# A hybrid decoder layer on one core: sums of activations spread over a product, rotary tables in pieces in a slab of plain products, and turnings at the ends of stages placed between products

## The chip, the cores and the metric

The kernel runs on one core of one Trainium2 chip. The metric is the device time of one execution in microseconds, as the median over several executions. The kernel before takes 1881.18 us (three runs, 1879.79 to 1882.1).

## The reference

One layer on 256 tokens of width 2048, all in fp32, with a feed-forward part ("FFN") at either end:

```
x1 = x  + 1/2 * SwiGLU_1(RMSNorm(x))          # hidden width 5632
h  = RMSNorm(x1);  P = h @ w_in               # one projection for three groups of heads
     A: gated linear attention (4 heads)      B: sparse attention (8 heads, rotary, gathered blocks)
     C: cross attention into 256 memory tokens (4 heads)
x2 = x1 + concat(A, B, C) @ w_out
x3 = x2 + 1/2 * SwiGLU_2(RMSNorm(x2))
y  = RMSNorm(x3)

def swiglu(x, w_gate, w_up, w_down):
    return (jax.nn.silu(x @ w_gate) * (x @ w_up)) @ w_down
```

## The kernel before

**Stages.** First FFN, the mix (the three groups of heads), the output projection, second FFN. The weights come in from memory once, as pieces of 128x1024 in fp32 (tile `r`, a pool `raw` of 11). `split` (L283 to L290) cuts each into a high part, a copy to fp32r by ScalarE (`h`, L288), and a low part, a subtraction by VectorE (`l`, L289). Each product is then three matmuls, high with high, high with low, low with high (`mm3`, L301 to L304). So each piece of weights costs ScalarE a copy, VectorE a subtraction, and TensorE 6 or 12 matmuls of 128x512.

**An FFN.** The hidden width is cut into 11 slabs of 512. Slab 0 (`first_slab`, L404) makes the gate product and the up product plainly: 8 pieces of 12 matmuls each, for both halves of the tokens. Between the two stands `combine` (L352 to L379): it makes from the activations `hh`, `hl` the four sums that the later slabs multiply (tiles `sh`, `sl`): four adds (`whole`, L360), four sums of those (L369, L372, L374, L377), and four splits of the result (copy L365, subtraction L366), each on 128x1024. Slabs 1 to 10 (`slab`, L438) do three quarters of their depth as seven products in place of eight (`SEVENS` = 3: sums of weights by VectorE, L481, L483, L485, and an adding DMA on GpSimd's queue, L473) and one quarter plainly; that is 25 steps and 174 matmuls a slab, with VectorE putting blocks together afterwards (L493 to L496, L506, L508, L510, L512) and the activation at L507, L509, L511, L513.

**What is filled in.** The down product of slab s-1 runs inside slab s. After steps 2 and 4 (`TURNS`) the hidden values are turned (`hidden`, L388: four transposes L391, a copy L393 to the high part of `gx`, a subtraction L394 to its low part). After the steps listed in `FILLS` come eight "fills" of 12 matmuls each (L425), all into one PSUM bank `px`, each followed by an add to `acc` on VectorE (L402). In slab 10 the last two fills (`LATE` = 2) come after the slab's own products; then the hidden values of slab 10 itself are turned, and its down product runs plainly (L531 to L549).

**What else stands there.** `prepare` (L573) makes the rotary tables with some sixty small VectorE operations of 128x192 (L587 to L604), 128x128 and 128x64 (L613 to L615); it is called once, after step 10 of slab 1. After each quarter j of the width of the first FFN's last down product, and of the output projection, `square_acc` (L342) sums squares on ScalarE, and `transposed` (L334) turns that quarter of `acc` (transposes L339, split L330 and L331) into the input of the next stage (`xh`, `xl` for the mix, whose first product is `agq`, L688; `zh`, `zl` for the second FFN).

**Order.** Each engine runs its instructions in one fixed order. A scheduler fixes it when the program is built: it goes by the program's order as a priority, and by its own estimate of when an instruction could start. A wait at the head of an engine's order holds up all behind it.

## Time and profile before

| | |
|---|---|
| median of three runs | 1881.18 us (1879.79 to 1882.1) |
| the profiled execution | 1881.27 us, of which the span in the profile is 1879.5 us |
| TensorE busy | 1840.5 us, 98% of the span |
| VectorE busy | 1642.3 us, 87% |
| ScalarE busy | 1086.0 us, 58% |
| GpSimd busy | 84.6 us, 5% |
| read from memory | 393.68 MB, 211 GB/s over the span |

Busy means that at least one instruction of the engine was running. TensorE is cut in two: PE is the matmul itself, PEld the load of its weights, which overlaps. Matmuls overlap each other too: one lasts about 0.39 us, and the next starts before it ends. A stretch in which TensorE counts as busy all the time can still be slow where the granted clock is low.

### The profile page before, as it was taken

What the parts mean: (1) busy time and instruction counts of PE and PEld (TensorE: products, weight loads), DVE (VectorE), ACT (ScalarE), POOL (GpSimd) and SP (SyncE); (2) the same over time, 40 slices, a digit from 0 to 9 for tenths busy, and PEclk for the clock granted to TensorE, in tenths of its full rate; (3) what the DMA queues carried; (4) which work ended last, traced back from release to release, by engine and by line L of the source; (5) the groups of instructions that cost most, each with busy time, mean ns of one, the idle gap of its engine ahead of it and who ended that gap; (6) DMA issues with size and microseconds to landing.
All of it is one profiled execution on the core that took longest, in us unless ns stands there. A gap on an engine that the chain in (4) does not pass through costs nothing.

```text
span 1879.5 us, 23784 instructions
## 1 busy us (share of the span) xinstructions
PE 1840.5 (98%) x8465; PEld 1486.1 (79%) x8465; DVE 1642.3 (87%) x2101; ACT 1086.0 (58%) x1376; POOL 84.6 (5%) x109
## 2 busy tenths in 40 slices
PE   8989999999999999999999999999999999999997
PEld 5868888888888877777777787888888888888885
DVE  7999999999999985576577854999999999999995
ACT  7446665656565656533456744566556655666563
POOL 0000000000000000001010000000000000000000
PEclk9999999999999999999999999999999999999999
DMA  9768777767776754545744453876777677767771
GB/s 333 228 190 261 253 225 235 247 202 226 236 249 197 229 169 158 188 150 177 247 157 130 163 181 117 295 239 209 213 237 255 203 214 238 253 201 216 239 246 49
DMA packets 111655, 397.34 MB, mean 211 GB/s; under 512 B 12592, under 2 KB 12848, under 8 KB 111408
## 3 DMA queue, kind: packets, MB, share of 16 engines
q1 hardware_dynamic: 102896, 364.36, 55.4%
q0 software_dynamic: 8640, 31.46, 9.7%
q8 instruction: 66, 1.08, 0.2%
q14 instruction: 53, 0.43, 0.1%
HBM read 393.68 MB, written 2.10 MB: 211 GB/s over the span
## 4 chain that ended last, share of the span: by engine, by line
PE 91%; DVE 5%; ACT 1%; issue 1%; POOL 1%; ACTq 0%; POOLq 0%; DVEq 0%
PE pm L303 20%; PE pm L302 20%; PE pm L304 20%; PE px L303 8%; PE px L302 8%; PE px L304 8%; DVE l L289 1%; PE pt L391 1%; PE pm L854 1%; PE px L819 0%; POOL y L326 0%; PE pt L339 0%; DVE exg L910 0%; PE po L1047 0%; POOL y L325 0%
## 5 line engine op out<-in xcount | busy, mean ns | idle before, releaser
L288 ACT ACTIVATE h<-r 128x1024 fp32r<-128x1024 f32 (+1 forms) x838 | 877.8, 1052 | 660.3 <-PE pm L304 491.6
L289 DVE TENSOR_TENSOR l<-r,h 128x1024 fp32r<-128x1024 f32 (+1 forms) x838 | 990.7, 1207 | 137.7 <-ACT h L288 129.3
L303 PE MATMUL px<-l,gx 128*128 128x512 f32 x624 | 243.2, 390 | 1.7 <-DVE l L289 1.7
L302 PE MATMUL px<-h,gx 128*128 128x512 f32 x624 | 243.2, 390 | 0.0
L304 PE MATMUL px<-h,gx 128*128 128x512 f32 x624 | 242.9, 389 | 0.0
L303 PE MATMUL pm<-l,sh 128*128 128x512 f32 x480 | 191.9, 400 | 2.3 <-DVE l L289 2.3
L302 PE MATMUL pm<-h,sh 128*128 128x512 f32 x480 | 190.1, 397 | 0.3 <-ACT h L288 0.3
L304 PE MATMUL pm<-h,sl 128*128 128x512 f32 x480 | 188.0, 392 | 0.0
L303 PE MATMUL pm<-l,hh 128*128 128x512 f32 x364 | 144.8, 398 | 3.6 <-DVE l L289 3.6
L302 PE MATMUL pm<-h,hh 128*128 128x512 f32 x364 | 142.4, 395 | 4.4 <-ACT h L288 4.4
L303 PE MATMUL pm<-l,zh 128*128 128x512 f32 x364 | 144.3, 396 | 0.1
L302 PE MATMUL pm<-h,zh 128*128 128x512 f32 x364 | 143.3, 394 | 0.0
L304 PE MATMUL pm<-h,zl 128*128 128x512 f32 x364 | 142.2, 391 | 0.0
L304 PE MATMUL pm<-h,hl 128*128 128x512 f32 x364 | 142.2, 391 | 0.0
L303 PEld LDWEIGHTS px<-l,gx 128*128 128x128 f32 x624 | 117.2, 188 | 26.7 <-DVE l L289 2.4
L302 PEld LDWEIGHTS px<-h,gx 128*128 128x128 f32 x624 | 117.2, 188 | 25.4 <-ACT h L288 0.2
L304 PEld LDWEIGHTS px<-h,gx 128*128 128x128 f32 x624 | 117.2, 188 | 24.2
L303 PE MATMUL pm<-l,xh 128*128 128x512 f32 (+2 forms) x320 | 120.7, 377 | 1.5 <-DVE l L289 1.5
L302 PE MATMUL pm<-h,xh 128*128 128x512 f32 (+2 forms) x320 | 121.3, 380 | 0.0
L304 PE MATMUL pm<-h,xl 128*128 128x512 f32 (+2 forms) x320 | 121.0, 379 | 0.0
L402 DVE SCALAR_TENSOR_TENSOR acc<-px,acc 128x512 f32<-128x512 f32 x156 | 106.9, 685 | 8.3 <-PE px L304 7.9
L302 PEld LDWEIGHTS pm<-h,sh 128*128 128x128 f32 x480 | 90.6, 189 | 20.5 <-ACT h L288 0.9
(329 smaller groups left out, 2641.0 us busy)
## 6 DMA issues: line engine op xcount, KB each, us to landing
r<-ffn1u SPq DMA_DIRECT2D x88, 512.0 KB, 4.9
r<-ffn1d SPq DMA_DIRECT2D x88, 512.0 KB, 4.9
r<-ffn2u SPq DMA_DIRECT2D x88, 512.0 KB, 4.7
r<-ffn2d SPq DMA_DIRECT2D x88, 512.0 KB, 4.8
r<-ffn1g SPq DMA_DIRECT2D x87, 512.0 KB, 5.0
r<-ffn2g SPq DMA_DIRECT2D x87, 512.0 KB, 5.1
r<-wout SPq DMA_DIRECT2D x32, 512.0 KB, 3.4
r<-ffn1u POOLq DMA_DIRECT2D x30, 512.0 KB, 7.3
```

Source lines behind the costliest of these rows:

```text
L288: act.activation(h[:, sl], r[:, sl], AF.Copy)
L289: dve.tensor_sub(l[:, sl], r[:, sl], f(h[:, sl]))
L302: pe.matmul(out, ah, wh, start=first, stop=False)
L303: pe.matmul(out, ah, wl, start=False, stop=False)
L304: pe.matmul(out, al, wh, start=False, stop=last)
L391: pe.transpose(pt[:, k], g[:, k * 128:k * 128 + 128], ident)
L402: dve.scalar_tensor_tensor(a, pd, 0.5, a, op0=ALU.mult, op1=ALU.add)
L854: pe.matmul(pcs[n][32 * p:32 * p + 32], flats[n][:, c * 4 + p], r[:, p * 256:p * 256 + 256], start=c == 0, stop=c == 7, tile_position=(0, ...
```

## The change

1. `combine` gives out its work as eight steps, and `product` calls one before each of the eight pieces of the up product, in both FFNs.
2. Slab 1 of the first FFN is made plain (`plain=(1,)`, no sevens): 16 steps of 12 matmuls, no sums of weights, no adding DMAs, and at its end two activations straight from PSUM and two multiplications. Its turnings and fills have their own places (`PLAIN_TURNS`, `PLAIN_FILLS`).
3. `prepare` is a generator, and one piece of it is called after each step of slab 1.
4. In slab 10 three fills are late, and the two turnings stand between them; the turned values go into a tile "gl" of their own in place of `gx`.
5. The sums of squares and the turning of the last quarter (j = 3), with the norm that needs it, move into the next stage's first product, before its piece 1.

```diff
-LATE = 2
+LATE = 3
+PLAIN_TURNS = (1, 2)
+PLAIN_FILLS = (3, 5, 6, 8, 9, 11, 12, 14)
...
-        def whole(k0, t0):
-            x = raw().rearrange("p (k t) -> p k t", k=8)
+        x = {}
+
+        def whole(n, k0, t0):
+            x[n] = raw().rearrange("p (k t) -> p k t", k=8)
             q = (slice(None), slice(k0, k0 + 8), slice(t0, t0 + 128))
-            dve.tensor_add(x, f(th[q]), f(tl[q]))
-            return x
-
-        def put(i, x):
+            dve.tensor_add(x[n], f(th[q]), f(tl[q]))
+
+        def put(i, n, op, a, b):
+            getattr(dve, op)(x[n], x[a], x[b])
             h, l = (v[:, 4 * i:4 * i + 4].rearrange("p a (b t) -> p (a b) t", b=2) for v in (sh, sl))
-            act.activation(h, x, AF.Copy)
-            dve.tensor_sub(l, x, f(h))
-
-        x21, x22 = whole(0, 128), whole(8, 128)
-        dve.tensor_sub(x22, x21, x22)
-        put(0, x22)
-        x11 = whole(0, 0)
-        dve.tensor_sub(x21, x11, x21)
-        put(2, x21)
-        dve.tensor_sub(x22, x22, x11)
-        put(1, x22)
-        x12 = whole(8, 0)
-        dve.tensor_add(x12, x12, x22)
-        put(3, x12)
-        return sh, sl
-
-    def ffn(name, th, tl, r, after, before=lambda i: None, by_rows=None):
+            act.activation(h, x[n], AF.Copy)
+            dve.tensor_sub(l, x[n], f(h))
+
+        return (sh, sl), [lambda: whole(21, 0, 128), lambda: whole(22, 8, 128),
+                          lambda: put(0, 22, "tensor_sub", 21, 22), lambda: whole(11, 0, 0),
+                          lambda: put(2, 21, "tensor_sub", 11, 21), lambda: put(1, 22, "tensor_sub", 22, 11),
+                          lambda: whole(12, 8, 0), lambda: put(3, 12, "tensor_add", 12, 22)]
+
+    def ffn(name, th, tl, r, after, before=lambda i: None, by_rows=None, plain=()):
...
-        def hidden_tiles():
-            x = sbuf("gx", "gx", F32R).rearrange("p (a k t) -> p a k t", a=2, k=4)
+        def hidden_tiles(last=False):
+            if last:
+                x = t16("gl").rearrange("p (a k) t -> p a k t", a=4)
+            else:
+                x = sbuf("gx", "gx", F32R).rearrange("p (a k t) -> p a k t", a=2, k=4)
             return x[:, 0], x[:, 1]
...
-            s4 = combine(th, tl)
-            product(pu, th, tl, wu[0])
+            s4, made = combine(th, tl)
+            product(pu, th, tl, wu[0], lambda c: made[c]())
...
-                if first:
-                    banks[n] = mbank() if n == "x22" else bank()
+                if first and n not in banks:
+                    banks[n] = mbank() if n == "x22" and sevens else bank()
...
             def behind():
                 for w in work.pop(steps[0], ()):
                     w()
-                if steps[0] == 10:
-                    before(("gate", s))
+                before((s, steps[0]))
                 steps[0] += 1
...
-            for u in range(SEVENS):
+            for u in range(sevens):
                 b11, b12, b21, b22 = quarter(u)
                 nc.gpsimd.dma_start(b12, wu[s, u + 4], accum_op=ALU.add)
...
-            p1, u2, d12, d22 = (t512("c") for _ in range(4))
-            act.activation(p1, banks["p1"], AF.Copy)
-            dve.tensor_add(u2, banks["p6"], p1)
-            dve.tensor_sub(d12, banks["q5"], u2)
-            dve.tensor_add(u2, banks["p7"], u2)
-            dve.tensor_sub(d22, banks["q5"], u2)
-            for u in range(SEVENS, 4):
+            if sevens:
+                p1, u2, d12, d22 = (t512("c") for _ in range(4))
+                act.activation(p1, banks["p1"], AF.Copy)
+                dve.tensor_add(u2, banks["p6"], p1)
+                dve.tensor_sub(d12, banks["q5"], u2)
+                dve.tensor_add(u2, banks["p7"], u2)
+                dve.tensor_sub(d22, banks["q5"], u2)
+            for u in range(sevens, 4):
...
-                        times(top, A_(half, 0), u, w, False, last)
-                        times(bottom, A_(half, 1), u, w, bottom == "x22" and u == SEVENS and half == 0, last)
+                        times(top, A_(half, 0), u, w, u == half == 0, last)
+                        times(bottom, A_(half, 1), u, w,
+                              half == 0 and u == (sevens if bottom == "x22" else 0), last)
                         behind()
+            if not sevens:
+                gs = []
+                for t, (g, v) in enumerate((("p2", "q3"), ("p4", "x22"))):
+                    y, z = t512("c"), t512("c")
+                    act.activation(y, banks[g], AF.Silu, scale=rr(t))
+                    dve.scalar_tensor_tensor(z, banks[v], rr(t), y, op0=ALU.mult, op1=ALU.mult)
+                    gs.append(z)
+                return gs
...
             g2 = hidden_tiles()
             fills = [w for j in range(4) for w in down_fill(s - 1, g2, j)]
-            work = {at: [lambda t=t, gs=gs, g2=g2: hidden(gs[t], *g2, t)] for t, at in enumerate(TURNS)}
+            turns, places = (PLAIN_TURNS, PLAIN_FILLS) if s in plain else (TURNS, FILLS)
+            work = {at: [lambda t=t, gs=gs, g2=g2: hidden(gs[t], *g2, t)] for t, at in enumerate(turns)}
             n = len(fills) - (LATE if s == SLABS - 1 else 0)
-            for at, w in zip(FILLS, fills[:n]):
+            for at, w in zip(places, fills[:n]):
                 work.setdefault(at, []).append(w)
-            gs = slab(s, s4, work)
-            for w in fills[n:]:
-                w(bank())
+            gs = slab(s, s4, work, 0 if s in plain else SEVENS)
+
         s = SLABS - 1
-        g2 = hidden_tiles()
-        for t in range(2):
-            hidden(gs[t], *g2, t)
+        g2 = hidden_tiles(True)
+        for i, w in enumerate(fills[n:]):
+            w(bank())
+            if i < 2:
+                hidden(gs[i], *g2, i)
...
         dve.memset(tot, 0.0)
+        yield
...
                 dve.tensor_add(tot, tot, q1)
+                yield
...
         frac(q1, q1)
+        yield
...
             dve.tensor_scalar_mul(sing[n][:, :, 64:], sing[n][:, :, 64:], -1.0)
+            yield
...
+    def norm_and_turn1(j):
+        square_acc(ss1, j)
+        transposed(j, C["mixg"], st1["h"], st1["l"])
+
     def after1(j):
         if j == 0:
             st1["h"], st1["l"] = t16("xh"), t16("xl")
-        square_acc(ss1, j)
-        transposed(j, C["mixg"], st1["h"], st1["l"])
+        if j < 3:
+            norm_and_turn1(j)
...
-        elif at == ("gate", 1):
-            prepare()
-        elif at == ("gate", 3):
+        elif at[0] == 1:
+            next(prep, None)
+        elif at == (3, 10):
             norm_mem()
 
-    ffn("ffn1", hh, hl, r1, after1, before1)
+    prep = prepare()
+    ffn("ffn1", hh, hl, r1, after1, before1, plain=(1,))
     xh, xl = st1["h"], st1["l"]
-
-    r2 = keep.tile([128, 2], F32, name="r2")
-    dve.tensor_copy(r2, finish_ss(ss1))
-    rm = keep.tile([128, 2], F32, name="rm")
-    dve.tensor_copy(rm, finish_ss(ssm))
-    r2q = keep.tile([128, 2], F32, name="r2q")
-    dve.tensor_scalar_mul(r2q, r2, 0.125)
-    r2n = keep.tile([128, 2], F32, name="r2n")
-    dve.tensor_scalar_mul(r2n, r2, -1.0)
+    r2, rm, r2q, r2n = (keep.tile([128, 2], F32, name=n) for n in ("r2", "rm", "r2q", "r2n"))
+
+    def last_of_ffn1(c):
+        if c == 1:
+            norm_and_turn1(3)
+            dve.tensor_copy(r2, finish_ss(ss1))
+            dve.tensor_copy(rm, finish_ss(ssm))
+            dve.tensor_scalar_mul(r2q, r2, 0.125)
+            dve.tensor_scalar_mul(r2n, r2, -1.0)
...
-    b = proj("agq")
+    b = proj("agq", last_of_ffn1)
...
+    def norm_and_turn2(j):
+        square_acc(ss2, j)
+        transposed(j, C["g2"], zh, zl)
+
     for j in range(4):
         pd = [bank(), bank()]
         product(pd, oh, ol, A["wout"][j])
...
             dve.tensor_add(a, pd[t], a)
         if zh is None:
             zh, zl = t16("zh"), t16("zl")
-        square_acc(ss2, j)
-        transposed(j, C["g2"], zh, zl)
+        if j < 3:
+            norm_and_turn2(j)
     r3 = keep.tile([128, 2], F32, name="r3")
-    dve.tensor_copy(r3, finish_ss(ss2))
+
+    def before2(at):
+        if at == 1:
+            norm_and_turn2(3)
+            dve.tensor_copy(r3, finish_ss(ss2))
...
-    ffn("ffn2", zh, zl, r3, after2, by_rows=finish)
+    ffn("ffn2", zh, zl, r3, after2, before2, by_rows=finish)
```

The first place is the up product of slab 0 on VectorE, in the first FFN. `r` are pieces of weights, and where L360 to L377 write them, sums of activations; `sh`, `sl` are the split sums; `l` is the low part of a piece of weights, for which TensorE waits. Before:

```order
L360 TENSOR_TENSOR r<-hh,hl 128x1024
L366 TENSOR_TENSOR sl<-r,sh 128x1024
L372 TENSOR_TENSOR r<-r 128x1024
L374 TENSOR_TENSOR r<-r 128x1024
L289 TENSOR_TENSOR l<-r,h 128x1024
L366 TENSOR_TENSOR sl<-r,sh 128x1024 x2
L377 TENSOR_TENSOR r<-r 128x1024
L289 TENSOR_TENSOR l<-r,h 128x1024 x2
L366 TENSOR_TENSOR sl<-r,sh 128x1024
L289 TENSOR_TENSOR l<-r,h 128x1024 x5
```

and with the change (L363 is L360 of before, L366 the sums of L369 to L377, L369 is L366, L291 is L289):

```order
L369 TENSOR_TENSOR sl<-r,sh 128x1024
L291 TENSOR_TENSOR l<-r,h 128x1024 x2
L363 TENSOR_TENSOR r<-hh,hl 128x1024
L1074 TENSOR_SCALAR neg<-kept 128x16 x2
L366 TENSOR_TENSOR r<-r 128x1024 x2
L363 TENSOR_TENSOR r<-hh,hl 128x1024
L291 TENSOR_TENSOR l<-r,h 128x1024
L369 TENSOR_TENSOR sl<-r,sh 128x1024
L291 TENSOR_TENSOR l<-r,h 128x1024
L369 TENSOR_TENSOR sl<-r,sh 128x1024
L291 TENSOR_TENSOR l<-r,h 128x1024 x2
L366 TENSOR_TENSOR r<-r 128x1024
```

The subtractions for the weights now stand between the sums, where before only one stood among the first eight operations after the norm.

The second place is VectorE at the start of slab 1, from the two multiplications that end slab 0 (L418 before, L416 now). Operations of 128x192 and `posf` belong to the rotary tables. Before:

```order
L418 SCALAR_TENSOR_TENSOR g<-pm,r_124,sil 128x512 x2
L289 TENSOR_TENSOR l<-r,h 128x1024 x3
L591 MEMSET r 128x192
L289 TENSOR_TENSOR l<-r,h 128x1024
L394 TENSOR_TENSOR gx<-pt,gx 128x4x128
L582 CAST posf<-posi 128x3
L289 TENSOR_TENSOR l<-r,h 128x1024
L587 TENSOR_TENSOR r<-r,posf 128x192
L481 TENSOR_TENSOR r<-r 128x1024
```

and with the change:

```order
L416 SCALAR_TENSOR_TENSOR g<-pm,r_124,sil 128x512 x2
L591 CAST posf<-posi 128x3
L291 TENSOR_TENSOR l<-r,h 128x1024
L596 TENSOR_TENSOR r<-r,posf 128x192
L633 CAST maskb<-r 128x128
L598 CAST r<-r 128x192
L633 CAST maskb<-r 128x128
L599 TENSOR_TENSOR r<-r 128x192
L610 TENSOR_SCALAR r<-r 128x192
L604 TENSOR_SCALAR r<-r 128x192
L605 TENSOR_SCALAR r<-r 128x192
```

After those rows come nine more small operations on the tables, a low part of turned values (`gx`) and two more on the tables, before the next subtraction L291. So 19 operations on tables and masks and one on `gx` stand between the first two subtractions of the list, where before two small ones and one on `gx` stood among five.

The third place is VectorE where slab 1 ends and slab 2 begins. L614, L613, L615 write the rotary tables; L508 to L513 end slab 1. Before:

```order
L613 TENSOR_TENSOR ckn_83<-r 128x64
L615 TENSOR_SCALAR skn_82<-skn_82 128x2x64
L614 TENSOR_TENSOR skn_84<-r 128x64
L613 TENSOR_TENSOR ckn_83<-r 128x64
L614 TENSOR_TENSOR skn_84<-r 128x64
L508 TENSOR_TENSOR c<-pm,c 128x512
L615 TENSOR_SCALAR skn_84<-skn_84 128x64
L512 TENSOR_TENSOR c<-px,c 128x512
L509 SCALAR_TENSOR_TENSOR c<-c,r_124 128x512
L513 SCALAR_TENSOR_TENSOR c<-c,r_124 128x512
L483 TENSOR_TENSOR r<-r 128x1024
L289 TENSOR_TENSOR l<-r,h 128x1024
```

and with the change (L510 multiplies the hidden values of slab 1, L478, L480, L482 are the sums of weights of slab 2, L400 the adds after fills):

```order
L400 SCALAR_TENSOR_TENSOR acc<-px,acc 128x512
L291 TENSOR_TENSOR l<-r,h 128x1024 x2
L478 TENSOR_TENSOR r<-r 128x1024
L400 SCALAR_TENSOR_TENSOR acc<-px,acc 128x512
L291 TENSOR_TENSOR l<-r,h 128x1024
L480 TENSOR_TENSOR r<-r 128x1024
L291 TENSOR_TENSOR l<-r,h 128x1024
L482 TENSOR_TENSOR r<-r 128x1024
L400 SCALAR_TENSOR_TENSOR acc<-px,acc 128x512
L510 SCALAR_TENSOR_TENSOR c<-pm,r_124,c 128x512
L291 TENSOR_TENSOR l<-r,h 128x1024
L510 SCALAR_TENSOR_TENSOR c<-pm,r_124,c 128x512
```

The tables' operations are gone from there, and one operation for each half of the tokens is left to end the slab.

## Rows read from the trace of the kernel before

**Rows 1.** The page's part 1 (busy time of each engine over the whole span, its share, instructions) and the first line of part 4 (the chain of work that ended last, by engine).

```profile
PE 1840.5 (98%) x8465; PEld 1486.1 (79%) x8465; DVE 1642.3 (87%) x2101; ACT 1086.0 (58%) x1376; POOL 84.6 (5%) x109
...
PE 91%; DVE 5%; ACT 1%; issue 1%; POOL 1%; ACTq 0%; POOLq 0%; DVEq 0%
```

**Rows 2.** Windows: the span cut into stretches. Columns: from:to, length in us, then for PE, PEld, DVE, ACT and POOL the busy us and instructions, the mean granted TensorE clock, the DMA share, GB/s.

```profile
28.00:61.00 33.00, 27.45 (x109) 21.26 (x110) 31.02 (x34) 20.22 (x23) 3.71 (x4) 0.95 0.94 325
61.00:129.00 68.00, 65.28 (x282) 51.38 (x282) 66.82 (x116) 37.06 (x39) 2.59 (x3) 1.00 0.64 188
129.00:150.00 21.00, 16.16 (x63) 12.53 (x62) 20.31 (x39) 8.19 (x10) 0.86 (x1) 0.84 0.71 215
150.00:690.00 540.00, 540.00 (x2401) 445.17 (x2400) 524.74 (x536) 330.34 (x336) 20.70 (x24) 1.00 0.73 231
690.00:712.00 22.00, 19.75 (x84) 15.49 (x83) 14.87 (x19) 9.91 (x15) 0.00 (x0) 0.92 0.20 61
712.00:745.00 33.00, 31.17 (x181) 25.56 (x180) 20.20 (x41) 20.49 (x42) 3.64 (x6) 1.00 0.45 152
...
1165.00:1185.00 20.00, 18.34 (x74) 13.48 (x73) 14.73 (x19) 10.79 (x17) 0.89 (x2) 0.91 0.80 305
1185.00:1840.00 655.00, 655.00 (x2912) 539.68 (x2911) 631.08 (x641) 396.17 (x399) 25.94 (x30) 1.00 0.71 228
1840.00:1856.00 16.00, 13.74 (x64) 10.73 (x63) 10.74 (x14) 6.55 (x10) 0.00 (x0) 1.00 0.00 1
```

**Rows 3.** The timeline (start us, us, engine, line, operation, out<-in, count, and in brackets the idle time before it with what ended it) of TensorE and VectorE around the up product of slab 0. The matmul at 53.96 and that at 60.60 are the first and the last of 30 in a row.

```profile
35.32 0.73 PE L302 MATMUL pm<-h,hh 128*128 128x512 f32 x2 [3.29 <-ACT h L288]
...
37.39 0.79 PE L303 MATMUL pm<-l,hh 128*128 128x512 f32 x1 [1.33 <-DVE l L289]
...
53.96 0.39 PE L302 MATMUL pm<-h,hh 128*128 128x512 f32 x1
...
60.56 1.41 DVE L418 SCALAR_TENSOR_TENSOR g<-pm,r,sil 128x512 f32<-128x512 f32 x2
...
60.60 0.39 PE L304 MATMUL pm<-h,hl 128*128 128x512 f32 x1
```

**Rows 4.** Windows with the same columns as rows 2, four short stretches.

```profile
35.00:38.00 3.00, 1.34 (x4) 0.81 (x5) 3.00 (x4) 2.98 (x4) 0.00 (x0) 0.81 0.34 117
135.00:143.00 8.00, 5.72 (x17) 4.49 (x17) 7.67 (x9) 2.85 (x4) 0.00 (x0) 0.57 0.42 156
702.00:706.00 4.00, 3.69 (x11) 3.08 (x12) 0.94 (x2) 0.60 (x1) 0.00 (x0) 0.57 0.02 9
1173.00:1177.00 4.00, 3.88 (x10) 2.46 (x10) 3.75 (x6) 4.00 (x7) 0.00 (x0) 0.57 1.02 415
```

**Rows 5.** Groups of VectorE instructions between 61 and 129 us, which is nearly the whole of slab 1: line, shapes, count, busy us, mean ns of one, idle time before them.

```profile
L289 DVE TENSOR_TENSOR l<-r,h 128x1024 fp32r<-128x1024 f32 x30 | 36.3, 1218 | 0.5 <-ACT h L288 0.4
L402 DVE SCALAR_TENSOR_TENSOR acc<-px,acc 128x512 f32<-128x512 f32 x8 | 5.5, 686 | 0.3
L481 DVE TENSOR_TENSOR r<-r 128x1024 f32<-128x1024 f32 x3 | 3.7, 1219 | 0.0
...
L596 DVE TENSOR_TENSOR r<-r 128x192 f32<-128x192 f32 x10 | 3.5, 351 | 0.1
L595 DVE TENSOR_SCALAR r<-r 128x192 f32<-128x192 f32 x11 | 2.8, 254 | 0.1
```

**Rows 6.** The waits of TensorE over the whole run: the waiting matmul's line, what it waited for, us in total, times, longest us.

```profile
PE pm L303 <- DVE l L289: 7.4, 9, 2.3
...
PE px L303 <- DVE l L289: 1.7, 1, 1.7
...
PE pt L339 <- DVE xl L331: 1.3, 3, 0.5
```

**Rows 7.** The timeline from the end of slab 1 into slab 2.

```profile
129.50 0.69 DVE L614 TENSOR_TENSOR skn<-r 128x128 f32<-128x128 f32 x3
...
132.33 0.68 DVE L508 TENSOR_TENSOR c<-pm,c 128x512 f32<-128x512 f32 x1
...
133.63 0.74 DVE L509 SCALAR_TENSOR_TENSOR c<-c,r 128x512 f32<-128x512 f32 x1
...
134.43 0.66 PE L391 MATMUL pt<-ident,c 128*128 128x128 f32 x4 [2.56 <-DVE c L509]
...
136.09 1.22 DVE L289 TENSOR_TENSOR l<-r,h 128x1024 fp32r<-128x1024 f32 x1
...
137.36 0.79 PE L303 MATMUL pm<-l,sh 128*128 128x512 f32 x1 [2.28 <-DVE l L289]
```

**Rows 8.** The timeline at the three ends of stages: of the first FFN, of the output projection, of the second FFN.

```profile
700.56 0.50 PE L302 MATMUL pm<-h,gx 128*128 128x512 f32 x1 [1.24 <-ACT gx L393]
...
702.31 1.03 PE L391 MATMUL pt<-ident,c 128*128 128x128 f32 x4 [1.01 <-DVE gx L394]
...
1171.77 0.62 ACT L288 ACTIVATE h<-r 128x512 fp32r<-128x512 f32 x1
...
1172.08 0.83 PE L339 MATMUL pt<-ident,acc 128*128 128x128 f32 x4 [1.20 <-DVE zl L331]
...
1845.82 0.50 PE L302 MATMUL pm<-h,gx 128*128 128x512 f32 x1 [1.24 <-ACT gx L393]
...
1847.57 0.66 PE L391 MATMUL pt<-ident,c 128*128 128x128 f32 x4 [1.02 <-DVE gx L394]
```

More of the change, by code (lines that the diff above doesn't have):

```diff
@@ L436, in down_fill, with slab @@
             return [lambda pd=None: fill(0, pd), lambda pd=None: fill(1, pd)]
-        def slab(s, s4, work):
+        def slab(s, s4, work, sevens):
             sh, sl = (v.rearrange("p (q a) (b t) -> p q (a b) t", q=4, b=2) for v in s4)
@@ L469, in quarter @@
                 return b11, b12, b21, b22
-            for u in range(SEVENS):
+            for u in range(sevens):
                 b11, b12, b21, b22 = quarter(u)
                 nc.gpsimd.dma_start(b12, wu[s, u + 4], accum_op=ALU.add)
-                first, last = u == 0, u == SEVENS - 1
+                first, last = u == 0, u == sevens - 1
                 def product7(n, left, x, ends=False):
```

## The prediction

> **What bounds the kernel now.** I began with the busy shares and the chain of waits: TensorE is busy 98% of the span and stands for 91% of the chain [rows 1]. So time can be won only where TensorE waits, or where its clock is low, and every matmul that is added costs. Then I cut the span into windows [rows 2]. In the long middle of both FFNs, 150 to 690 and 1185 to 1840 us, TensorE is busy without a gap; what is lost lies in short stretches: around the up product of slab 0, in slab 1, from slab 1 into slab 2, and at the ends of stages. VectorE is the engine that is late there: it is busy 31.02 of 33 us, 66.82 of 68 and 20.31 of 21 in the first three windows. The timeline at those places shows which wait ends last [rows 3, 7, 8], and short windows show where the clock falls [rows 4].
>
> Two unit prices. A matmul in an undisturbed row starts 0.229 us after the one before: 29 steps from 53.96 to 60.60 [rows 3]. A split's subtraction takes 1.218 us on VectorE, the add after a fill 0.686 [rows 5].
>
> A stall costs more than itself in places. Over 135 to 143 us the granted clock is 0.57 on average, and so it is in the four us after 702 and after 1173 [rows 4]: there TensorE ran mostly at 1.2 GHz, half its upper level. All three follow waits of more than 1 us. 8 us with a mean of 0.57 lose about 0.43 x 8 = 3.4 us, and four us lose 1.7. The stall at 35 us is followed by a low clock too [rows 4]: 0.95 over the first window's 33 us [rows 2], which loses about 1.6.
>
> **The change, part by part.** The sum is made against the profiled execution, 1881.27 us with a span of 1879.5; the median of the runs is 1881.18, so the two may be taken as one.
>
> *Up product of the first FFN.* Before, VectorE does nearly all of `combine` ahead of the product's weights, and TensorE waits 3.29 us at 35.32 and 1.33 at 37.39 [rows 3]; with the 1.6 us of the low clock that is 6.3. The work is not less, it is spread: 8 splits and 12 operations on sums, 20 x 1.218 = 24.4 us of VectorE against 96 x 0.229 = 22.0 us of TensorE. So VectorE still falls behind by at most 2.4 us, less what was split ahead during the gate product. Walking through the new order, the fourth piece of weights is late: three operations on sums and two splits stand ahead of it. I take 1.0 us for that. The multiplication that needs the product, at 60.56 before, should then come at about 55.0: **-5.5**, between -3 and -6.3.
>
> *Slab 1, plain.* 16 steps of 12 in place of 174 matmuls: 18 more, 18 x 0.229 = **+4.1**. What TensorE loses there now: 68 us hold 282 instructions, which at the rate of the undisturbed window (540 us for 2401, 0.225 each) would take 63.4 [rows 2], so 4.6 are lost, of which 1.7 is one fill's wait [rows 6] and the rest mostly small idle times. VectorE's load falls: 24 splits in place of 33, no sums of weights (9 x 1.219), no blocks to put together. 24 x 1.218, eight adds, two multiplications, the low parts and some 14 to 21 us of tables make 52 to 59 us against 67 of TensorE (288 x 0.229 and the turnings). But the order is worse at one point: 19 operations of 0.25 to 0.35 us [rows 5] and one low part, about 6 us, stand between two splits at the start. TensorE uses a piece per 2.75 us and has three or four pieces in hand, so I expect one stall of about 1.1 us near step 4. The fills are the second point. They share one bank; after steps 5 and 6, 8 and 9, 11 and 12 they follow each other with only 2.75 us of other products between, and the add that frees the bank stands on VectorE behind two splits: 2 x 1.218 + 0.686 = 3.1 us, plus up to one split under way. I take 1.1 us once, and nothing for the other pairs, since by then VectorE is ahead. New stalls 2.2, old losses 4.6 gone: **-2.4** beside the +4.1; new stalls could be 0.5 to 10. The three adding DMAs that go from GpSimd's queue, and the sooner loads on SyncE's, cost nothing: the DMA share in that window is 0.64 [rows 2], and 16 steps of 2.75 us ask for their weights at no higher rate than 25 shorter ones.
>
> On that bank the trace of before shows one fill of slab 1 that waits 1.7 us, for a split [rows 6], with fills two short steps apart. The Trainium skill ("Perfetto Trace Analysis", on optimizing Tensor performance) says that independent groups of matmuls should rotate through different PSUM banks, so that emptying one overlaps the next; that speaks against fills after adjacent steps into one bank. Taken strictly, all three pairs would wait 1.1 us, and the sum below would come out 2.2 us higher.
>
> *From slab 1 into slab 2.* Operations on tables run on VectorE from 129.5 on, ahead of the four that end slab 1; L509 ends only at 134.4, TensorE waits 2.56 us for it and 2.28 for a split that was pushed behind [rows 7], and the low clock adds 3.4: 8.2. By the count of instructions (63 x 0.225 = 14.2 of 21 us) it is 6.8. I take 7.5. With the change the tables are done by then and one activation and one multiplication follow each bank's last matmul, while slab 2's first products need neither. I leave 0.2 of it: **-7.3**, between -5 and -8.2.
>
> *End of the first FFN.* The waits of 1.24 and 1.01 us for the turned values [rows 8] and the low clock behind them, 1.7, make 4.0. Now a fill of 12 matmuls (2.75 us) stands behind each turning, longer than the copy and the subtraction of 0.6 and 0.7 us with a split ahead. Slab 10 in turn has one fill less to cover its last steps and two more pieces of weights held: 0.5. **-3.5**, between -2 and -4.
>
> *The last quarter's norm into the next product.* Three waits of the transposes L339, 1.3 us in all [rows 6], lie in the norm before `agq`: 12 matmuls of the next product now run ahead. **-1.0**, between 0 and -1.8. Before the second FFN the transposes wait 1.20 us at 1172.08, but the copy of the first weights starts only at 1171.77 [rows 8], since they land with the stage: the moved transposes leave TensorE waiting for that instead. I take **-0.4**, between +0.5 and -1.8. The row of the clock after 1173 then stays as it is.
>
> *Second FFN.* Its up product stands in a window without a gap [rows 2], so spreading gains nothing there; the cover is that VectorE runs ahead. At its end the waits are 1.24 and 1.02, with the granted clock at 1.00 [rows 2, 8]: 2.3, less 0.3 in slab 10: **-2.0**, between -0.5 and -2.6.
>
> Sum: -5.5 + 4.1 - 2.4 - 7.3 - 3.5 - 1.0 - 0.4 - 2.0 = -18.0, so **1863.3 us**. With all low ends it is about 1856.5, with all high ends about 1881.
>
> **The rivals.**
>
> *The clock eats half.* Left-over stalls of about 1 us, one in the up product and two in slab 1, might each be followed by some four us at the lower clock, as at 702 [rows 4]: 3 x 1.7 = 5.1, so about 1868.5. For it: four of the stalls of before were paid twice. Against it: the window of slab 1 has a mean granted clock of 1.00 in spite of its 1.7 us wait, and so has the end of the second FFN [rows 2, 6]. The Trainium skill ("TensorE: Matmul & The Clock Gate", part 1) has the lower clock as the default and activity as what releases it, by which any stall may be paid twice; the trace bears that out at four of the six places named here.
>
> *The ends give nothing.* The turnings between fills could move the wait to the first down product, and the moved norm could make `agq` wait for its own bank or for the activations. Then 3.5, 1.0 and 2.0 are lost and it ends at about 1869.8. Against it: ScalarE and VectorE are both idle at those ends, VectorE 14.87 of 22 us busy [rows 2].
>
> *Slower: every fill of slab 1 waits.* If the splits of the fills queue behind those of the steps and the tables, all eight fills meet a wait as the one of before, 1.7 us [rows 6], each followed by the low clock for 1.7: 8 x 3.4 = 27 us in place of 2.2, and 1863.3 + 25 = 1888. It decides from (18.0 + 3.8 + 2.2) / 8 = 3.0 us per fill. For it: VectorE was busy 66.82 of 68 us and one operation more may tip it. Against: its load in this slab falls to below 60.
>
> *The change does not do what it says.* The scheduler could order the engines as before. The orders show otherwise at the first three places, so this holds at most for the second FFN, where little is at stake; but if the gain of the first places only moved VectorE's lateness into slab 2, the time would stay near 1880.
>
> **How the numbers follow.** My forecast has 0.62, the clock 0.18, the ends 0.12, slower 0.04, unchanged 0.04. The range takes in the first three, and leaves out the last two and the outer ends of the bounds: 1856 to 1872. A difference of 0.2%, about 3.8 us, is what a measurement of this kernel can tell from no change. The first three cases are all faster: 0.92; same 0.04, slower 0.04.
>
> **What would show it.** Right: the multiplication after the up product near 55 us, no wait over 0.5 us between slab 1 and slab 2 and a clock of 1.00 there, no wait of TensorE for turned values at the two ends of FFNs, and slab 1 about 67 us long plus two stalls of about 1. Wrong: waits of TensorE on L289's successor or on the fills' bank in slab 1 that sum to more than 6 us, a clock below 1.00 in slab 1, or new waits in slab 2, where there were none.

## The result and the profile after

The changed kernel takes 1858.65 us (median of four runs, 1857.22 to 1859.58) against 1881.64 of the kernel before in the same comparison: a ratio of 0.9876, 95% interval 0.9863 to 0.9888, 23.0 us faster. Forecast were 1863.3 us and a range of 1856 to 1872. The profiled spans are 1879.5 and 1857.7 us.

Windows of the changed kernel, at the places of those of before (columns as in [rows 2]):

```profile
28.00:56.00 28.00, 26.54 (x114) 20.87 (x113) 26.89 (x31) 20.35 (x26) 1.90 (x2) 1.00 0.76 280
56.00:124.00 68.00, 68.00 (x304) 55.98 (x303) 60.04 (x121) 29.55 (x32) 1.92 (x2) 1.00 0.72 238
124.00:145.00 21.00, 21.00 (x98) 17.31 (x97) 20.96 (x22) 14.37 (x16) 0.86 (x1) 1.00 0.76 231
680.00:692.00 12.00, 12.00 (x58) 9.93 (x57) 9.93 (x12) 5.33 (x6) 0.00 (x0) 1.00 0.16 48
692.00:725.00 33.00, 32.50 (x187) 26.62 (x186) 21.60 (x42) 22.20 (x46) 3.64 (x6) 1.00 0.37 130
1149.00:1169.00 20.00, 17.95 (x73) 13.49 (x72) 14.63 (x19) 12.76 (x19) 0.89 (x2) 0.91 0.82 308
1820.00:1835.00 15.00, 15.00 (x69) 12.30 (x69) 12.59 (x15) 7.31 (x11) 0.00 (x0) 1.00 0.00 1
```

Slab 1, the way into slab 2 and both ends of FFNs now have TensorE busy from end to end at the full granted clock; only the start of the second FFN (the sixth line) has kept its loss. The waits of TensorE over the whole run (columns as in [rows 6]) show the same: the long waits on a split, on turned values and on `px` are gone, the one on `zl` is not.

```profile
PE pm L304 <- ACT h L290: 3.0, 4, 0.9
PE pm L305 <- DVE l L291: 2.9, 6, 1.0
PE pt L341 <- DVE zl L333: 1.3, 1, 1.3
```

The timeline at the places of [rows 3, 7, 8]:

```profile
55.83 1.44 DVE L416 SCALAR_TENSOR_TENSOR g<-pm,r,sil 128x512 f32<-128x512 f32 x2 [0.23 <-PE pm L306]
...
121.78 0.75 DVE L510 SCALAR_TENSOR_TENSOR c<-pm,r,c 128x512 f32<-128x512 f32 x1
...
123.57 0.75 DVE L510 SCALAR_TENSOR_TENSOR c<-pm,r,c 128x512 f32<-128x512 f32 x1
...
127.07 0.60 PE L386 MATMUL pt<-ident,c 128*128 128x128 f32 x4
...
683.13 0.60 PE L386 MATMUL pt<-ident,c 128*128 128x128 f32 x4
...
1152.91 0.44 PE L341 MATMUL pt<-ident,acc 128*128 128x128 f32 x2 [1.30 <-DVE zl L333]
...
1822.68 0.60 PE L386 MATMUL pt<-ident,c 128*128 128x128 f32 x4
```

The values of slab 1 are ready at 124.3, 2.7 us before the turning at 127.07 asks for them; before, TensorE waited 2.56 us for them [rows 7].

To set every run side by side, each span is cut at the same events of its timeline: A, the second multiplication after the up product; B, the first turning in slab 3; C, the first in slab 10; D, the first transpose of the norm behind the first FFN; E, that behind the output projection; F, the second multiplication in the second FFN; G, the second turning in its slab 10. Lengths in us, worked out from start times; the parts are numbered as in the change.

| kernel (parts) | to A | A-B, slabs 1, 2 | B-C | C-D, end of FFN 1 | D-E, mix | E-F | F-G | G-end | span |
|---|---|---|---|---|---|---|---|---|---|
| before (none) | 61.2 | 141.7 | 437.5 | 69.8 | 391.0 | 118.1 | 569.7 | 90.5 | 1879.5 |
| changed (1 to 5) | 56.5 | 133.1 | 437.4 | 65.3 | 389.7 | 118.3 | 569.7 | 87.7 | 1857.7 |
| e1 (1) | 56.1 | 148.2 | 437.5 | 68.3 | 391.5 | 118.1 | 569.7 | 90.5 | 1879.7 |
| e2 (2) | 61.4 | 133.1 | 437.4 | 69.8 | 391.3 | 118.0 | 569.7 | 90.4 | 1871.1 |
| e3 (3) | 61.5 | 138.8 | 437.5 | 69.7 | 391.6 | 117.9 | 569.7 | 90.5 | 1877.1 |
| e4 (4) | 62.0 | 141.7 | 437.5 | 65.3 | 392.0 | 117.1 | 569.7 | 87.8 | 1873.1 |
| e5 (5) | 62.7 | 141.7 | 437.5 | 68.3 | 389.6 | 118.0 | 569.7 | 92.0 | 1879.4 |
| e6 (1 to 5, fills adjacent) | 54.8 | 133.2 | 437.4 | 65.3 | 391.4 | 116.7 | 569.7 | 87.9 | 1856.4 |
| e7 (1, 4, 5, tables over 8 slabs) | 56.2 | 134.4 | 448.4 | 65.3 | 389.6 | 116.7 | 569.7 | 88.1 | 1868.4 |
| e8 (1 to 5, pools in another order) | 55.2 | 133.1 | 437.4 | 65.3 | 391.5 | 118.3 | 569.7 | 87.7 | 1858.2 |
| e9 (1, 2, 4, 5) | 56.4 | 132.9 | 437.4 | 65.3 | 389.8 | 117.8 | 569.7 | 87.7 | 1857.0 |
| e10 (1 to 5, early weights) | 55.1 | 133.1 | 437.4 | 65.3 | 389.4 | 117.6 | 569.7 | 88.0 | 1855.6 |
| e11 (2 to 5) | 62.0 | 133.1 | 437.4 | 65.3 | 389.7 | 118.9 | 569.7 | 88.0 | 1864.1 |

Segments whose code two kernels share agree within 0.3 us in A-B, B-C and F-G; "to A", D-E and E-F differ by up to 2 us between runs of the same code, and C-D and G-end by 1.5 where the clock falls in one run and not in the other, so only larger differences are read there.

"To A" hides a part of the gain, since the changed kernel's profiled execution came late to the place where the change begins. All runs have a wait of 0.36 to 0.38 us for ScalarE at the head of the gate product's last piece; here it is before and with the change:

```profile
28.10 0.73 PE L302 MATMUL pm<-h,hh 128*128 128x512 f32 x2 [0.37 <-ACT h L288]
```

```profile
29.84 0.74 PE L304 MATMUL pm<-h,hh 128*128 128x512 f32 x2 [0.37 <-ACT h L290]
```

From there to the multiplication after the up product (60.56 [rows 3] and 55.83) it was 32.5 us and is 26.0, which is 6.5 us less, where "to A" has 4.7. Over all runs that way takes 32.5 to 33.3 us without the first part and 26.0 to 26.7 with it, and the place itself comes at 27.9 to 28.7 and at 28.1 to 29.8 us.

### The profile page after: what moved, and what is told of

It reads as the page before. It is cut to its first block, busy times and chain, and to the rows that moved or that the text cites. A ratio compares the mean times of both kernels' runs of the same rounds, so it can differ in the third digit from the quotient of the medians.

```text
span 1857.7 us, 23760 instructions
## 1 busy us (share of the span) xinstructions
PE 1834.4 (99%) x8483; PEld 1484.8 (80%) x8483; DVE 1620.5 (87%) x2075; ACT 1076.5 (58%) x1366; POOL 82.3 (4%) x106
## 3 DMA queue, kind: packets, MB, share of 16 engines
q1 hardware_dynamic: 102896, 364.36, 56.5%
## 4 chain that ended last, share of the span: by engine, by line
PE 92%; DVE 4%; ACT 1%; DMA 1%; POOL 1%; issue 1%; SPq 0%; ACTq 0%; POOLq 0%; DVEq 0%
PE pm L305 21%; PE pm L304 21%; PE pm L306 20%; PE px L305 8%; PE px L304 8%; PE px L306 8%; PE pt L386 1%; DMA r<-ffn1g 1%; DVE l L291 1%; PE pm L872 1%; POOL y L328 0%; PE px L837 0%; PE pt L341 0%; DVE exg L928 0%; PE po L1065 0%
## 5 line engine op out<-in xcount | busy, mean ns | idle before, releaser
L290 ACT ACTIVATE h<-r 128x1024 fp32r<-128x1024 f32 (+2 forms) x829 | 869.8, 1052 | 654.0 <-PE pm L306 492.6
L291 DVE TENSOR_TENSOR l<-r,h 128x1024 fp32r<-128x1024 f32 (+2 forms) x829 | 982.5, 1207 | 137.6 <-ACT h L290 127.7
L304 PE MATMUL px<-h,gx 128*128 128x512 f32 x616 | 239.6, 389 | 0.0
L306 PE MATMUL px<-h,gx 128*128 128x512 f32 x616 | 239.5, 389 | 0.0
L305 PE MATMUL pm<-l,sh 128*128 128x512 f32 x456 | 180.9, 397 | 0.0
L304 PE MATMUL pm<-h,sh 128*128 128x512 f32 x456 | 180.6, 396 | 0.0
L306 PE MATMUL pm<-h,sl 128*128 128x512 f32 x456 | 177.5, 389 | 0.0
L305 PE MATMUL pm<-l,hh 128*128 128x512 f32 x398 | 157.3, 395 | 1.6 <-DVE l L291 1.6
L304 PE MATMUL pm<-h,hh 128*128 128x512 f32 x398 | 155.5, 394 | 3.0 <-ACT h L290 3.0
L306 PE MATMUL pm<-h,hl 128*128 128x512 f32 x398 | 154.5, 389 | 0.0
L400 DVE SCALAR_TENSOR_TENSOR acc<-px,acc 128x512 f32<-128x512 f32 x154 | 105.6, 686 | 7.7 <-PE px L306 7.6
L304 PEld LDWEIGHTS pm<-h,sh 128*128 128x128 f32 x456 | 85.7, 188 | 18.6
```

The costliest lines, as they stand in the source:

```text
L290: act.activation(h[:, sl], r[:, sl], AF.Copy)
L291: dve.tensor_sub(l[:, sl], r[:, sl], f(h[:, sl]))
L304: pe.matmul(out, ah, wh, start=first, stop=False)
L305: pe.matmul(out, ah, wl, start=False, stop=False)
L306: pe.matmul(out, al, wh, start=False, stop=last)
L400: dve.scalar_tensor_tensor(a, pd, 0.5, a, op0=ALU.mult, op1=ALU.add)
```

## The experiments

**e1, spread sums alone.** Against the changed kernel: parts 2 to 5 undone. Kept is

```
-            product(pu, th, tl, wu[0])
+            product(pu, th, tl, wu[0], lambda c: made[c]())
```

> The kernel before with the first part alone: the sums of activations given out before each piece of the up product, in both FFNs. Theory A (the parts add up, each paying at its own place): the multiplication after the up product comes 4.7 us earlier, as in the changed kernel, nothing of it is lost behind, and the whole run is 4.7 us shorter (about 1877). Theory B (VectorE's lateness only moves): slab 1 is still made with sevens and VectorE is busy 66.8 of 68 us there, so the 4.7 us are handed back in slab 1 and at its end, and the run is within 1.5 us of before.

Measured: 1883.1 us against 1880.86, ratio 1.0011 (1.0001 to 1.0020): slower by 0.1%, if at all. The product ends 5.2 us earlier, and slabs 1 and 2 take 6.6 us more. Theory B, and more than it asked. Windows of e1, slab 1 and two stretches in it:

```profile
61.00:129.00 68.00, 59.94 (x239) 45.82 (x238) 63.78 (x126) 31.20 (x34) 1.73 (x2) 0.92 0.58 183
66.00:76.00 10.00, 10.00 (x46) 8.15 (x44) 10.00 (x11) 5.73 (x7) 0.00 (x0) 1.00 0.15 52
86.00:96.00 10.00, 4.54 (x14) 2.45 (x13) 9.29 (x23) 3.06 (x4) 0.00 (x0) 0.79 0.63 227
```

VectorE is busy all of 66 to 76 us while almost nothing is loaded: the loads wait on SyncE's queue, one of them 8.7 us, for pieces that VectorE has not yet split. Twenty us later the split weights are late and TensorE works less than half the time, at a lower clock. Its longest wait there is for a split that stands on VectorE behind operations on the tables:

```profile
90.99 0.50 PE L305 MATMUL pm<-l,hh 128*128 128x512 f32 x1 [3.16 <-DVE l L291]
```

Part 1 alone gains nothing.

**e2, the plain slab alone,** the tables in one go after step 10.

```
-    ffn("ffn1", hh, hl, r1, after1, before1)
+    ffn("ffn1", hh, hl, r1, after1, before1, plain=(1,))
```

> The kernel before with slab 1 of the first FFN plain (its own places for turnings and fills), the tables made in one go after step 10 as before. If VectorE's total load in slab 1 is what made the stalls there and behind it, the plain slab alone brings all of the 8.6 us that slab 1 and the way into slab 2 gave in the changed kernel: about 1872.5. If the place of the tables' operations is what counts, they stand again in front of the end of the slab, a stall of 2 us or more stays between slab 1 and slab 2 with a low clock behind it, and the gain is 2 to 5 us: 1876 to 1879.

Measured: 1873.65 us, ratio 0.9964 (0.9951 to 0.9977). A-B falls by 8.5 us, as in the changed kernel. What decides is VectorE's load beside TensorE's time, and not where the program calls the tables. Windows of e2:

```profile
61.00:129.00 68.00, 68.00 (x303) 55.65 (x302) 58.62 (x120) 29.24 (x31) 1.91 (x2) 1.00 0.59 185
129.00:150.00 21.00, 21.00 (x97) 17.30 (x96) 20.95 (x22) 14.32 (x16) 0.85 (x1) 1.00 0.80 240
```

No gap is left in TensorE, with the tables still called in one go; VectorE runs them between 76 and 113 us, among the splits, well before the slab ends. A plain slab also has no adding DMAs, and gives TensorE 18 matmuls more to do meanwhile; no run separates these two from VectorE's smaller load.

**e3, the pieces alone,** in a slab 1 with sevens.

```
-        elif at == (1, 10):
-            list(prep)
+        elif at[0] == 1:
+            next(prep, None)
```

> The kernel before with the tables given out in 16 pieces after the first 16 steps of slab 1, which is still made with sevens (174 matmuls, no 18 more). If the place is what counts, the two stalls between slab 1 and slab 2 and the low clock behind them go (7 to 8 us) and no matmuls are added: 1873 to 1874, better than the plain slab. If the load counts, VectorE, busy 66.8 of 68 us already, is only late at other steps of slab 1: gain between 0 and 3 us, 1878 to 1881.

Measured: 1879.31 us, ratio 0.9994 (0.9984 to 1.0003); A-B 2.9 us shorter. The load theory again: the stalls behind slab 1 are gone, but slab 1 pays. Windows of e3, and the wait of TensorE between 61 and 150 us that makes most of it:

```profile
61.00:129.00 68.00, 60.89 (x260) 48.66 (x259) 66.85 (x127) 34.53 (x36) 2.61 (x3) 0.95 0.71 223
129.00:150.00 21.00, 21.00 (x98) 17.29 (x97) 20.73 (x24) 13.78 (x15) 0.86 (x1) 1.00 0.72 202
```

```profile
PE pm L305 <- DVE l L291: 4.8, 1, 4.8
```

VectorE is busy 66.85 of 68 us as before; the lateness has only moved forward. In matmuls and transposes, TensorE gets through 35 more than before in the second window (98 against 63) and 22 fewer in the first (260 against 282 [rows 2]): at 0.229 us each, 8.0 us won and 5.0 lost.

**e4, turnings between late fills alone,** in both FFNs.

```
-        for t in range(2):
-            hidden(gs[t], *g2, t)
+        for i, w in enumerate(fills[n:]):
+            w(bank())
+            if i < 2:
+                hidden(gs[i], *g2, i)
```

> The kernel before with three late fills and the turnings between them, in both FFNs, and the last turned values in a tile of their own. If the parts add up: 4.5 us at the end of the first FFN and 2.7 at the end of the second, as in the changed kernel, about 1874.0. If slab 10's own last steps suffer from having one fill less and two pieces held, or the norm behind the first FFN takes the gain back (its first quarter then comes when ScalarE is busier): 3 to 5 us in all, 1876.5 to 1878.5.

Measured: 1874.77 us against 1880.86, ratio 0.9967 (0.9955 to 0.9978). C-D is 4.5 us shorter and G-end 2.6, the same as in the changed kernel: this part adds up, and in the changed kernel TensorE waits for nothing between 615 and 700 us, slab 10's own steps among them.

**e5, the last quarter's norm alone.**

```
-        norm_and_turn1(j)
+        if j < 3:
+            norm_and_turn1(j)
```

(and so for `norm_and_turn2`, each called before piece 1 of the next product)

> The kernel before with the fifth part alone: the last quarter's sums of squares and turning moved into the first product of the next stage, behind the first FFN and behind the output projection. If the parts add up: 1.3 us less behind the first FFN and 0.2 more before the second, so about 1880.4, which the timing alone cannot tell from no change; the trace should show the wait of 1.2 us before the second FFN still there, since the weights' copy on ScalarE is what comes late. If the turnings were what held the second FFN's start: that wait goes, with the low clock behind it, and it is 3 us or more faster.

Measured: 1881.33 us against 1882.11, ratio 0.9997 (0.9987 to 1.0006): not to be told from no change. The mix segment is 1.4 us shorter, the wait before the second FFN still 1.3 us. But e6 and e8 have this part and a mix of 391.4 and 391.5, with a wait of 1.8 and 1.2 us for the first activations behind `agq` in place of 0.2. So its size, 0 to 1.5 us, stays open.

**e6, all eight fills after adjacent steps.**

```
-PLAIN_FILLS = (3, 5, 6, 8, 9, 11, 12, 14)
+PLAIN_FILLS = (3, 4, 5, 6, 7, 8, 9, 10)
```

> The changed kernel with the eight fills of the plain slab after steps 3 to 10, each after an adjacent step, so that seven times the one bank is asked for again after 2.75 us. If VectorE's load decides (per step and fill it has two splits, one add and some four table operations, about 4.2 us against 5.5 us of TensorE): no wait on the bank, the same time as the changed kernel within 1.5 us, 1857 to 1860. If the single bank limits, as the rule on rotating banks has it, each of the seven pairs waits 0.4 to 1.1 us: 3 to 8 us more, 1861.5 to 1866.5.

Measured: 1858.24 us, ratio to before 0.9875 (0.9860 to 0.9890), the changed kernel's within its interval. TensorE has no wait at all in the slab:

```profile
56.00:124.00 68.00, 68.00 (x304) 55.98 (x303) 61.01 (x121) 31.12 (x33) 1.92 (x2) 1.00 0.75 246
```

The one bank is not what limits here. The rule of the Trainium skill ("Perfetto Trace Analysis", on optimizing Tensor performance) that independent groups should rotate through banks speaks against these places; the measurement decides, at least while VectorE has 7 of 68 us to spare. In e7, where VectorE itself is held up, a fill does wait for the bank.

**e7, sevens in all slabs, two pieces of the tables in each of slabs 1 to 8.**

```
-        elif at[0] == 1:
+        elif at[0] != "gate" and at[1] in (6, 18):
             next(prep, None)
...
-    ffn("ffn1", hh, hl, r1, after1, before1, plain=(1,))
+    ffn("ffn1", hh, hl, r1, after1, before1)
```

> The changed kernel without the plain slab: all slabs with sevens, and the tables' 16 pieces given out two to a slab over slabs 1 to 8, after steps 6 and 18 (three raw slots stay held for that long). If a piece of some 1 us fits into the slack that VectorE has in each slab (517 of 535 us busy in slabs 2 to 10), the 18 matmuls are saved without a stall, 4.1 us, but slab 1 with sevens starts with VectorE late from the up product and loses 2 to 4: 1856 to 1859. If VectorE has no slack where a piece lands, or the held slots delay the weights' loads, stalls come in several slabs, each some 1 us and some paid twice: 1862 to 1875.

Measured: 1872.41 us, ratio 0.9949 (0.9934 to 0.9964): 14 us slower than the changed kernel by the medians, 10.7 by the spans. Slabs 1 and 2, with nearly all of the tables out of them, take 134.4 us against 148.2 in e1, so in e1 it was the tables' operations in slab 1 that cost; and yet 1.3 us more than the plain slab with all of them. The rest is lost later, most of it in slab 3, where VectorE waits once for weights, between 200 and 226 us:

```profile
DVE r L478 <- DMA r<-ffn1u: 6.2, 1, 6.2
```

Behind that wait the add after a fill comes late, and the next fill stands still for the bank; this is TensorE's longest wait between 190 and 262 us:

```profile
PE px L304 <- DVE acc L400: 4.7, 1, 4.7
```

The load had waited on its queue 8.1 us for a slot of the tables' (the pieces of weights, the tables and `norm_mem` share the pool `raw`). Slabs 4 to 7 lost 0.6 to 0.9 us each: where VectorE is busy 97% of the time there is little room for a piece.

**e8, the second FFN's pools in another order in memory.**

```
-    stage("f2", FFN_SB, FFN_PS)
+    stage("f2", {n: FFN_SB[n] for n in ("lo", "raw", "hi", "gx", "wk")}, FFN_PS)
```

> The changed kernel with the pools of the second FFN in another order in memory (low parts, weights, high parts, rest), so that the first pieces of its weights no longer have to wait until the output projection's last matmuls have read what lies at the same place. In the changed kernel the second load of the second FFN waits on its queue from 1145.4 to 1150.5 us for a matmul, and the stage start loses about 5 us with a low clock behind it. If that wait is the cause, the weights' copies come before the last sums of squares, the stall of 1.3 us and the low clock go, and it is 2 to 5 us faster: 1854 to 1857. If the turning of the last quarter, and ScalarE's order, hold the start in any case: within 1.5 us of the changed kernel.

Measured: 1858.15 us, ratio 0.9877 (0.9862 to 0.9892), no better than the changed kernel. Its timeline at the start of the second FFN:

```profile
1152.39 0.46 ACT L332 ACTIVATE zh<-pt,gains 128x256 fp32r<-128x256 f32 x1
...
1152.74 0.62 ACT L290 ACTIVATE h<-r 128x512 fp32r<-128x512 f32 x1
...
1153.41 0.44 PE L341 MATMUL pt<-ident,acc 128*128 128x128 f32 x2 [1.31 <-DVE zl L333]
```

The loads were issued without the wait, the first at 1148.3 us with 2.6 us to its landing, but ScalarE has the squares and the turned values ahead of the first weights' copy at 1152.74: its order holds that copy. TensorE's wait is for the turned values.

**e9, all but the pieces:** the tables in one go after step 10 of the plain slab.

```
-        elif at[0] == 1:
-            next(prep, None)
+        elif at == (1, 10):
+            list(prep)
```

> The changed kernel with the tables made in one go after step 10 of the plain slab, everything else as changed. The plain slab alone, with the tables in one go, already gave as much in slab 1 and on the way into slab 2 (8.5 us) as the whole change did (8.6). If the load of VectorE and the raw slots decide, and the plain slab has room for the tables in any order, the pieces are worth nothing: 1857 to 1860. If the spread sums leave VectorE so late at the start of the plain slab that the tables' place matters after all, stalls of 1 to 3 us come back near the end of slab 1, paid twice where the clock falls: 1861 to 1865.

Measured: 1858.17 us, ratio 0.9869 (0.9853 to 0.9885), A-B 132.9. The pieces are worth nothing once the slab is plain; VectorE runs the tables between 76 and 116 us here.

**e10, the first two pieces of the second FFN's gate weights** loaded and split before the pools are switched.

```
+    ready = [chunk(A["ffn2g"][0][c]) for c in range(2)]
     stage("f2", FFN_SB, FFN_PS)
...
+            w = ready[c] if c < len(ready) else chunk(src[c], parts if c == 0 else 1)
```

> The changed kernel with the first two pieces of the second FFN's gate weights loaded and split with the pools of the stage before, ahead of the switch of pools. Another order of the pools did not help, since ScalarE has the sums of squares and the first turned values ahead of the copy of the first weights. Here the scheduler has the copy earlier, and the gate product's first 6 matmuls stand ahead of all but the first turning. If ScalarE's order is what holds the start of the second FFN: the stall of 1.3 us and the low clock behind it go, 3 to 5 us faster than the changed kernel, 1854 to 1856. If TensorE then waits as long for the second weights or for the acc of the output projection: within 1.5 us of it, 1857 to 1860.

Measured: 1860.11 us (1857.34 to 1861.43), ratio 0.9879 (0.9862 to 0.9897): not to be told from the changed kernel. Its waits of TensorE around that start are

```profile
PE pm L304 <- ACT h L290: 1.5, 1, 1.5
PE pt L342 <- DVE zl L334: 0.6, 1, 0.6
PE pm L305 <- DVE l L291: 0.5, 1, 0.5
```

in place of the one of 1.3 us: the next weights are late instead. E-F is 0.7 us shorter than in the changed kernel, whose clock fell there, but 0.9 longer than in e6 and e7, which have the old order and kept the clock, as e10 did. No version tried here beats the changed kernel clear of the noise.

**e11, all but the spread sums.**

```
-            product(pu, th, tl, wu[0], lambda c: made[c]())
+            for m in made:
+                m()
+            product(pu, th, tl, wu[0])
```

> The changed kernel with the sums of activations made in one go between the two products of slab 0, as before, in both FFNs; all else as changed. Spread alone won 5 us in the up product and lost 6.6 in slab 1 when that was made with sevens. If spreading pays once slab 1 is plain, this kernel loses what the up product gained, 4.7 to 5.5 us: 1863.5 to 1864. If the plain slab has absorbed part of it (VectorE has room there and the sums are needed only from slab 2 on), less: 1860 to 1862.5.

Measured: 1865.89 us, ratio 0.9910 (0.9894 to 0.9926): 7 us slower than the changed kernel by the medians, 6.4 by the spans. "To A" is back at 62.0, 5.5 us longer, and A-B is unchanged. With a plain slab behind it, spreading pays in full.

## Why the prediction was right, and where its steps were off

The direction and the order of the places were right: every gain lies in the windows that the prediction named, and the long middles of both FFNs did not move (437.4 and 569.7 us). Most terms were sized too cautiously, so the sum is 3.8 us short of the spans. Step by step, by the spans (together 21.8 us; the medians say 23.0):

- *Up product*: forecast -5.5, measured -4.7, with its multiplication at 55.83 in place of "about 55.0". That these lie so close is in part luck: the execution came 1.7 us late to the gate product's last piece, and from there on the part gave 6.5, a little more than the term's bound of 6.3. A late piece of weights is seen, but it costs 0.27 us (at 42.9) where the term took 1.0. What is left are two short waits on ScalarE where the two products meet, 0.37 us, which the kernel before has too, and 0.82. What the prediction did not say is that this gain hangs on the plain slab: alone it was handed back (e1), with it kept (e11).
- *Slab 1 and the way into slab 2*: +4.1 - 2.4 - 7.3 = -5.6 forecast, -8.6 measured. This is the term that was mis-sized most. The old losses were estimated well: 4.6 + 7.5 = 12.1, against 8.6 + 4.1 = 12.7 that came back. The new stalls, put at 2.2, did not come: TensorE is busy 68 of 68 us. The 19 operations on tables and one low part did take from 58.4 to 64.3 us between two splits, as feared, but TensorE had enough split pieces in hand, and the fills never waited, not even seven times in a row (e6).
- Its reason was half right. It gave the -7.3 to the tables leaving the end of the slab. e3 moved them and nothing else, and lost in slab 1 some 5 of the 8 us that it won behind it; e2 left them in one go and won everything. What counts is VectorE's load in that slab beside TensorE's time, which the prediction put at 52 to 59 us against 67 and which came out at 60 of 68.
- *End of the first FFN*: -3.5 forecast, -4.5 measured in this pair of runs; the 0.5 for slab 10's lost fill is not there. With the same waits e1 and e5 take 68.3 us there in place of 69.8, so 1.5 of the 4.5 is a low clock that does not come in every run, and 3.0 the part that does.
- *Norm in `agq`*: -1.0 against -1.3, within what that segment scatters. *Start of the second FFN*: -0.4 against +0.2: the wait stays, as said, but not for the reason given. The prediction has the first weights copied late "since they land with the stage"; in the trace of before the first load is issued at 1164.2 us and takes 3.3 to land, some 4 us before its copy at 1171.77. e8 and e10 point to ScalarE's order and, once that is changed, to the next weights.
- *End of the second FFN*: -2.0 against -2.7; both waits are gone, and the 0.3 taken off for slab 10 is not there.

The rivals: no stall was left that a low clock could follow in slab 1, the ends gave all of theirs (e4), and no fill waited. The mechanism of the last rival, VectorE's lateness that only moves, is real: it is e1 and e3. The plain slab is what kept it from deciding.

## What to carry to other kernels

When an engine that feeds TensorE is the late one, moving its work earlier or later mostly moves the stall; here it paid to give it less to do in that stretch, even though TensorE got 4 us more, and then the moves paid too. Test the parts of such a change together as well as alone: alone the medians moved by +2.2, -7.2, -1.6, -6.1 and -0.8 us, 13.4 us of gain in all, together 23. Work that TensorE waits for at the end of a stage belongs between independent products that are kept back for it.

## What the runs showed that was not expected

Whether a stall is paid twice differs between runs of the same code. At the end of the first FFN the same two waits, 1.24 and 1.01 us, were followed by the lower clock in the kernel before, in e2 and in e3, and not in e1 and e5. The windows of e1 and of e2 there:

```profile
690.00:712.00 22.00, 19.74 (x90) 15.28 (x90) 15.81 (x19) 10.46 (x16) 0.00 (x0) 1.00 0.08 28
```

```profile
690.00:712.00 22.00, 19.74 (x88) 14.97 (x87) 11.51 (x16) 11.46 (x24) 0.00 (x0) 0.92 0.21 73
```

TensorE is busy 19.74 us in both; the mean granted clock is 1.00 in the one and 0.92 in the other, worth 1.5 us. At the end of the second FFN, where the kernel before has 1.00, e5 met the lower clock behind the same two waits (0.92 between 1839 and 1861 us), and its G-end is 92.0 in place of 90.5. At the start of the second FFN the same wait of 1.3 us gave 0.91 in the changed kernel, e8, e9 and e11 and 1.00 in e5, e6 and e7. So a term for the clock is a chance, not a price. The Trainium skill ("TensorE: Matmul & The Clock Gate", part 1) has activity as what releases the lower clock; these runs agree that it follows waits, but not that it follows each.
